# Layer 1's two h parts in one 512-column product, context's x0 by an adding DMA, and layer 1's gate sums further apart

## The chip, the cores and the metric

The kernel runs on one core of a Trainium2 chip. Its engines run side by side, each through its own list of instructions in a fixed order: TensorE (PE in the profile, with its weight loads shown apart as PEld), VectorE (DVE), ScalarE (ACT), GpSimd (POOL) and SyncE (SP), which issues nearly all DMAs. The metric is the device time of one execution in microseconds (us). Before the change it is 1170.85 us, the median of three runs (1170.73 to 1172.37).

## The reference, cut to what matters

Two layers of one block. Each layer normalises two streams of 256 tokens and 2048 features, the latents `x` and the context `ctx`, scales and shifts them, and projects both by the same `w_in` (2048 by 5120). The projection's columns feed three branches (a gated MLP, attention and a Fourier mix); their outputs, 2048 wide, go through `w_out`, are normalised, gated, and added to the stream.

```python
for l in range(DEPTH):                       # DEPTH = 2
    h   = rmsnorm(x,   g_pre[l]) * (1.0 + scale[:, None]) + shift[:, None]
    h_c = rmsnorm(ctx, g_pre[l]) * (1.0 + scale_c) + shift_c
    proj, proj_c = h @ w_in[l], h_c @ w_in[l]
    ...
    y = rmsnorm(y @ w_out[l], g_post[l])
    x_new = x + gate[:, None] * y
    if not last:
        ...                                  # the same branches on proj_c
        ctx = ctx + gate_c * y_c
    x = x_new
return x
```

In the second layer (layer 1 in the code) the context gives only keys and values to the latents' attention. So that layer needs all columns of `w_in` for 256 latent tokens, and only the columns `k` and `v` for the 256 context tokens.

## The kernel before

**Products.** Every large product is made from float32 numbers split into a high and a low part, each of a type that TensorE takes in one pass. `mm3` (L383) makes one 128-row step of a product as three matmuls into the same PSUM tile: high by high (L384), high by low (L385), low by high (L386). The low by low part is left out. In `tunit` (L473) the stationary operand is a 128 x 128 piece of the weights (`whi`, `wlo`) and the moving operand is a piece of h (`hh`, `hl`), whose columns are tokens; 16 such steps make one *unit* of 128 output features. In layer 0 a unit moves 512 columns (both streams), in layer 1 it moves the 256 latent columns, and 512 only for the two units `k`. `hh[k]` and `hl[k]` are tiles of 128 x 512: latents in the first 256 columns, context in the last 256 (`LAT`, `CTX`).

**The units of layer 1, in order.** `a_v` (h stationary, 512 columns of weights moving) together with the first two heads of `a_u` (`start_av`, `start_au`); then `au2`, `au3`; four `cx` (Fourier), four `ag` and four `cg` (gates); two `k`; `v` (h stationary, 256 columns moving); eight `q`; eight `bg`. That is 30 latent units through `tunit` and two `k` units. After that `finish` (L834) makes the output projection with tokens on the partitions and writes the result.

**Weights.** `Stream` (L331) brings 512 KB of weights at a time (half a unit) by DMA into one of three `raw` buffers; ScalarE makes the high part (`whi`, L367) and VectorE the low part (`wlo`, L368), into four buffers each, up to three halves ahead of their use.

**Order.** TensorE's instructions run in the order in which the program writes them. Work that comes back to TensorE later is a generator in `later`; each `yield d` says after how many units of a planner's clock its next piece is put between the products. `tick` advances that clock by 0.0405 per 32 moved columns of a step (0.648 per 512). The instructions of the other engines are ordered by the compiler from priorities; `low(n)` makes a block wait for the next n instructions. Delays of importance here: `YF` for the Fourier branch, `YQ, YA, YB` for attention, `YT` for `finish`.

**The context's way into layer 1.** `after_start` (L966) starts `boundary_ctx` (L980) after `au3`. It runs `boundary(1, acc)` (L908): four DMAs bring `x0` of the context into `raw` buffers; column sums of the squares of the layer's output (`col_sums`, L424) give 1/rms, spread over the partitions by `bcast` (L431); then, for each of 16 feature tiles, VectorE multiplies `yo[k]` by it (L933) and adds `x0` (L934), ScalarE squares the result (L937), and after every second tile TensorE adds the two squares into `ps_rs` (L944). Four small matmuls (L952) end the sum, and a second `bcast` gives the 1/rms of the new stream. `make_h` (L445) then writes the context halves of `hh` and `hl`. The gates `ag`, `cg` and `bg` write into the context halves of `yo`, so they follow.

**Users of a unit.** `gate` (L732), `fourier` (L615), the activation at L745 and `rope` (L644, for `q` and `k`) read the unit's PSUM tile directly. Short-lived tiles of all of them share the tag `w2k`, seven buffers (L74).

**`finish`.** `gate1` (L254) turns layer 1's gate sums, which VectorE collected in four tiles, into rows on all partitions: per 512 columns one DMA of two rows, one float32 matmul with ones (L260), an add (L261) and a product (L262) on VectorE. `turn` (L838) transposes the latents (L847) in eight pieces. Both put their products between those of `ps_y`, through the two `ms` PSUM buffers.

Of the kernel before, what the change touches and what calls it, by code (L numbers as in the profile page):

```python
# [13 lines left out]
P = 128  # L14
# [13 lines left out]
def units():  # L28
    """(name, first column, columns, first k tile, k tiles): blocks of w_in of 128 x 2048 each."""
# [37 lines left out]
def trunk_kernel(ctx: ExitStack, tc: tile.TileContext, xT, xhalf, cT, wss, wsl, wmod, win, wout0, wout1, const, vec, rows,  # L67
# [24 lines left out]
    # ---- constants  # L92
# [17 lines left out]
    class low:  # L110
        """instructions that may wait for the next `n`."""
# [22 lines left out]
    # ---- modulation: columns [128, 16, stream] of scale, shift and gate  # L134
# [5 lines left out]
    def mod_cols(l, cb, ps8):  # L140
        """ps8 [128, 4, 2]: silu(c) @ w_mod for 512 columns of column block cb."""
# [54 lines left out]
    def mod_dve(l, cb, red):  # L196
        """red [128, 2, 16]: sums over the 32 partitions of each quadrant, transposed."""
# [38 lines left out]
    def mod_gate1():  # L236
        """products of silu(c) and the gate's columns of w_mod in layer 1, still to be summed over partitions."""
# [16 lines left out]
    def gate1():  # L254
        """(sum + b_mod) * g_post of layer 1's gate, on all partitions."""
        for c in range(4):
            r = sb([P, 2, 512], F32, "mraw", 2)
            DMA.dma_start(r, rows[None, :, c * 512:(c + 1) * 512].to_broadcast([P, 2, 512]))
            ps = ms_ps("gate")
            PE.matmul(ps, ones, g1[c], start=True, stop=True)  # L260
            V.tensor_tensor(out=g1[c], in0=r[:, 0], in1=ps, op=ALU.add)  # L261
            V.tensor_tensor(out=g1[c], in0=g1[c], in1=r[:, 1], op=ALU.mult)  # L262
            yield YT

# [11 lines left out]
    YF = [5.0, 2.8], [3.8, 3.4]  # L276
# [18 lines left out]
    # ---- work of other engines that hands products back to the tensor engine later  # L295
# [32 lines left out]
    # ---- weights: raw -> exact parts hi + lo, in halves of a unit, ahead of their use  # L328
# [59 lines left out]
    def part(w, c):  # L388
        """columns c of both parts; a part is a tile or a list of tiles side by side."""
# [19 lines left out]
    # ---- per-token reciprocal rms from sums over features  # L409
# [14 lines left out]
    def col_sums(ps, q, n, start=True, stop=True):  # L424
        """columns of ps: sums over the partitions of q [128, n * 128], one accumulation group."""
# [10 lines left out]
    # ---- streams in feature-major tiles  # L436
# [7 lines left out]

    def make_h(l, k, rb, streams):  # L445
        """h = x * rstd * gs + sh, as hi + lo; rb: rstd over the tokens of `streams`."""
# [6 lines left out]
        for s in streams:  # L453
            sl = slice(s * S, (s + 1) * S)
            first = A.activation(hh[k][:, sl], t[:, sl], AF.Identity, bias=sh[l][:, k, s:s + 1])  # L455
        for s in streams:
            sl = slice(s * S, (s + 1) * S)
            last = V.scalar_tensor_tensor(out=hl[k][:, sl], in0=t[:, sl], scalar=sh[l][:, k, s:s + 1],
                                          in1=hh[k][:, sl].bitcast(F32), op0=ALU.add, op1=ALU.subtract)
# [13 lines left out]
    def tunit(n, sl=None):  # L473
        """feature-major product of one unit of 128 columns: PSUM [128, n]."""
# [8 lines left out]
        return ps  # L483

# [10 lines left out]
    # ---- one layer, up to the inputs of the output projection  # L495
    def layer(l):
# [12 lines left out]
        # a_v (token-major) and two heads of a_u, k outermost  # L509
        av = [mm_ps("av") for _ in range(nt)]  # L510
        au = [mm_ps("au") for _ in range(2)]
        def start_av(k, ts):
            c = slice((k % 2) * 512, (k % 2 + 1) * 512)
            for t in ts:
                sl = slice(t * P, (t + 1) * P)
                mm3(av[t], (hh[k][:, sl], hl[k][:, sl]), part(avw, c), k == 0, k == KT - 1)

        def start_au(k):
            for j in range(2):
                c = slice((k % 4) * 256 + j * P, (k % 4) * 256 + (j + 1) * P)  # L520
                mm3(au[j][:, 0:n], part(auw, c), (hh[k][:, 0:n], hl[k][:, 0:n]), k == 0, k == KT - 1)
# [57 lines left out]
        # branch A  # L579
        def branch_a():  # L580
            vt = [w2k([P, 512]) for _ in range(nt)]
            ss = sb([P, 4], F32, "ss")
            for j in range(2):
                A.activation(ytmp(j), au[j][:, 0:n], AF.Gelu_apprx_tanh)
# [20 lines left out]
        # branch C  # L605
# [37 lines left out]
        # branch B  # L643
        def rope(hi, lo, ps):  # L644
            """x * cos + rot(x) * sin of the latents, and x of the context, as hi + lo."""
# [10 lines left out]
            if hi.shape[-1] > S:  # L656
                split_into(hi[:, CTX], lo[:, CTX], ps[:, S:T])
# [85 lines left out]
        for h in (2, 3):  # L743
            ps = tunit(n)
# [3 lines left out]
        for g in range(4):  # L748
            ps = tunit(n)
# [3 lines left out]
        for h in range(4):  # L753
            ps = tunit(n)
            gate(h, ps)
        state["phase"] = f"cg{l}"
        for g in range(4):
            ps = tunit(n)
# [6 lines left out]
        for j in range(2):  # L765
            ps = tunit(T)
            kt.append((sb([P, T], F32R, f"kt{j}"), sb([P, T], F32R, ("ws", "bsb")[j])))
            rope(*kt[j], ps)
# [3 lines left out]
        for k in range(KT):  # L772
# [3 lines left out]
            for t in range(4):  # L776
                ts = slice(t * P, (t + 1) * P)
                mm3(vps[t][:, 0:256], (hh[k][:, ts], hl[k][:, ts]), part(w, c), k == 0, k == KT - 1)
# [3 lines left out]
        for h in range(8):  # L782
            ps = tunit(n)
# [3 lines left out]
        for h in range(8):  # L787
            ps = tunit(n)
# [11 lines left out]
    # ---- output projection  # L800
# [7 lines left out]
    def out_proj():  # L808
# [14 lines left out]
        later.add(boundary(0, acc), 1.0)  # L823
# [10 lines left out]
    def finish():  # L834
        """layer 1's output projection with tokens on partitions, and x1 + gate * y / rms(y)."""
        x1 = {}

        def turn():  # L838
            """x1 of the latents to tokens on partitions: [128, token tile, 512] per 512 columns."""
# [12 lines left out]
        later.add(turn(), 2 * YT)  # L852
# [55 lines left out]
    def boundary(s, acc):  # L908
        """x1 = x0 + gate * y / rms(y) of stream s in place, and its own 1 / rms."""
# [185 lines left out]
```

## Time and profile before

| | us |
|---|---|
| three timed runs, median (lowest to highest) | 1170.85 (1170.73 to 1172.37) |
| span of the profiled execution | 1167.9 |
| median minus that span (start and end, outside the profile) | 2.95 |
| TensorE busy in the span | 1136.0 |
| VectorE / ScalarE / GpSimd busy | 881.8 / 509.8 / 17.3 |

Layer 0 takes the span up to about 757 us, layer 1's units run from there to about 1062 us, and `finish` to the end; the context's boundary lies between 808 and 848 us, `q` between 936 and 1002 us, with attention's last pieces up to 1036 us. TensorE's granted clock is 0.996 of full speed on average. A matmul's row in the profile lasts longer than TensorE needs for it, because matmuls overlap: how long one costs is read from the distance between the starts of successive rows.

### The profile page before, as it was taken

To read this page: it belongs to the slowest core of one execution; us is meant where nothing else is said; L and a number is where in the kernel's file an instruction comes from. 1 tells how busy PE (TensorE), PEld (TensorE's weight loads), DVE (VectorE), ACT (ScalarE), POOL (GpSimd) and SP (SyncE) were. 2 spreads that over 40 slices of the span, in tenths; PEclk is the share of its full clock that TensorE was granted. 3 is DMA by queue.
4 is the path that set the end of the run, shared out by engine and by line. 5 is a ranking of instruction groups with operands and counts; after the bars stand their busy time and mean duration, and the time that the engine had idled before them with its cause. 6 is when DMAs were issued, how large, how long until landed. Compare 5 with 4: busy or idle time off the path is not lost.

```text
span 1167.9 us, 17483 instructions
## 1 busy us (share of the span) xinstructions
PE 1136.0 (97%) x6656; PEld 953.7 (82%) x6656; DVE 881.8 (76%) x1469; ACT 509.8 (44%) x914; POOL 17.3 (1%) x23
## 2 busy tenths in 40 slices
PE   3999999999999999999999999999999999999996
PEld 1466688888898888888888888889899999997885
DVE  5454498888988878798989886495896678888554
ACT  4222513322224667632533233365563278745442
POOL 0000000000000000000000000200000000000001
PEclk9999999999999999999999999999999999999998
DMA  9999765466665334455466665365656665688563
GB/s 339 378 387 357 254 196 166 145 202 193 200 200 178 105 114 136 134 175 173 158 199 209 205 216 162 109 207 173 205 158 205 203 200 178 195 269 244 190 187 120
DMA packets 73892, 234.32 MB, mean 201 GB/s; under 512 B 8528, under 2 KB 9680, under 8 KB 73808
## 3 DMA queue, kind: packets, MB, share of 16 engines
q1 hardware_dynamic: 73808, 233.21, 61.6%
q8 instruction: 52, 0.85, 0.3%
q14 instruction: 32, 0.26, 0.1%
HBM read 231.08 MB, written 2.10 MB: 200 GB/s over the span
## 4 chain that ended last, share of the span: by engine, by line
PE 92%; DVE 3%; DMA 2%; ACT 2%; issue 1%; POOL 0%; SPq 0%; DVEq 0%; ACTq 0%; POOLq 0%
PE ps_t L384 20%; PE ps_t L385 20%; PE ps_t L386 20%; PE ps_mod L172 3%; PE ps_av L384 2%; PE ps_y L386 2%; PE ps_y L384 2%; PE ps_y L385 2%; PE ps_av L385 2%; PE ps_av L386 2%; PE ps_v L386 1%; PE ps_v L384 1%; PE ps_v L385 1%; PE ps_tp L722 1%; PE ps_au L384 1%
## 5 line engine op out<-in xcount | busy, mean ns | idle before, releaser
L384 PE MATMUL ps_t<-hh,whi 128*128 128x512 f32 (+1 forms) x1296 | 452.1, 349 | 0.0
L386 PE MATMUL ps_t<-hh,wlo 128*128 128x512 f32 (+1 forms) x1296 | 447.4, 345 | 0.0
L385 PE MATMUL ps_t<-hl,whi 128*128 128x512 f32 (+1 forms) x1296 | 447.0, 345 | 0.0
L367 ACT CAST whi<-raw 128x1024 fp32r<-128x1024 f32 x218 | 228.2, 1050 | 397.3 <-PE ps_t L385 274.4
L368 DVE TENSOR_TENSOR wlo<-raw,whi 128x1024 fp32r<-128x1024 f32 x218 | 265.3, 1220 | 99.1 <-ACT whi L367 98.8
L384 PEld LDWEIGHTS ps_t<-hh,whi 128*128 128x128 f32 x1296 | 244.9, 189 | 34.3 <-issue 4.6
L386 PEld LDWEIGHTS ps_t<-hh,wlo 128*128 128x128 f32 x1296 | 244.7, 189 | 30.6
L385 PEld LDWEIGHTS ps_t<-hl,whi 128*128 128x128 f32 x1296 | 244.9, 189 | 28.9 <-issue 0.5
L209 DVE SCALAR_TENSOR_TENSOR macc<-mraw,cs,macc 128x512 f32<-128x512 f32 x360 | 249.9, 745 | 17.6 <-DMA mraw<-in_wmod_dram 17.5
L455 ACT ACTIVATE hh<-w2k,sh 128x256 fp32r<-128x256 f32 x64 | 29.0, 502 | 61.4 <-DVE w2k L451 61.4
L384 PE MATMUL ps_y<-whi,hh 128*128 128x512 f32 x112 | 45.0, 401 | 0.0
L386 PE MATMUL ps_y<-whi,hl 128*128 128x512 f32 x112 | 43.8, 392 | 0.0
L385 PE MATMUL ps_y<-wlo,hh 128*128 128x512 f32 x112 | 43.7, 390 | 0.0
L384 PE MATMUL ps_av<-whi,hh 128*128 128x512 f32 x96 | 40.0, 416 | 0.0
L385 PE MATMUL ps_av<-wlo,hh 128*128 128x512 f32 x96 | 37.9, 395 | 0.4 <-DVE wlo L368 0.4
L172 PE MATMUL ps_mod<-hh,kt 128*32 128x512 f32 x64 | 21.5, 649 | 17.0 <-DMA hh<-in_wss_dram 17.0
L386 PE MATMUL ps_av<-whi,hl 128*128 128x512 f32 x96 | 37.6, 392 | 0.0
L386 PE MATMUL ps_v<-whi,hl 128*128 128x256 f32 x128 | 36.2, 283 | 0.0
L384 PE MATMUL ps_v<-whi,hh 128*128 128x256 f32 x128 | 36.2, 283 | 0.0
L385 PE MATMUL ps_v<-wlo,hh 128*128 128x256 f32 x128 | 36.2, 283 | 0.0
L468 DVE TENSOR_TENSOR acc<-acc,w2k 128x512 f32<-128x512 f32 (+1 forms) x33 | 21.2, 641 | 18.7 <-ACT w2k L467 17.2
L401 ACT CAST w2k<-ps_tp 128x512 fp32r<-128x512 f32 x40 | 23.5, 587 | 22.8 <-PE ps_scc L385 12.0
(292 smaller groups left out, 1491.8 us busy)
## 6 DMA issues: line engine op xcount, KB each, us to landing
raw<-in_win_dram SPq DMA_DIRECT2D x160, 512.0 KB, 4.1
mraw<-in_wmod_dram SPq DMA_DIRECT2D x128, 512.0 KB, 4.3
raw<-in_wout_dram SPq DMA_DIRECT2D x64, 512.0 KB, 4.2
hh<-in_wss_dram SPq DMA_DIRECT2D x32, 256.0 KB, 5.6
hl<-in_wss_dram SPq DMA_DIRECT2D x32, 256.0 KB, 5.4
yo<-in_xT_dram SPq DMA_DIRECT2D x16, 256.0 KB, 5.4
mraw<-in_wsl_dram SPq DMA_DIRECT2D x8, 512.0 KB, 6.9
yo<-in_wsl_dram SPq DMA_DIRECT2D x16, 256.0 KB, 7.2
```

Source lines behind the costliest of these rows:

```text
L172: PE.matmul(ps[32 * kk:32 * kk + 32, 0:n], cpad[:, kg * 4 + kk], ws[kk], start=kg == 0, stop=kg == 3, tile_position=(0, 32 * kk))
L209: V.scalar_tensor_tensor(out=acc[:, s], in0=w[:, kk % 2], scalar=c, in1=acc[:, s], op0=ALU.mult, op1=ALU.add)
L367: A.copy(ph, r[:, c])
L368: self.last = V.tensor_tensor(out=pl, in0=r[:, c], in1=ph.bitcast(F32), op=ALU.subtract)
L384: PE.matmul(ps, st[0], mv[0], start=start, stop=False)
L385: PE.matmul(ps, st[0], mv[1], start=False, stop=False)
L386: PE.matmul(ps, st[1], mv[0], start=False, stop=stop)
L401: A.copy(hi, src)
L455: first = A.activation(hh[k][:, sl], t[:, sl], AF.Identity, bias=sh[l][:, k, s:s + 1])
L468: V.tensor_tensor(out=acc[:, sl], in0=acc[:, sl], in1=q[:, sl], op=ALU.add)
L722: PE.transpose(tp[:, (2 * j + b) * P:(2 * j + b + 1) * P], src, ident)
```

## The change

1. In layer 1, `hh[k]` holds the latents' high part and low part side by side (256 + 256 columns), and `hl[k]` the same for the context (`h_of`). A latent step is then two matmuls (`mm2`): `whi` by all 512 columns, and `wlo` by the high part, added to the first 256 columns. Afterwards `joined` copies the second half of the PSUM tile to a `w2k` tile on ScalarE and adds the first half on VectorE. All 30 latent units, the two heads in `start_au`, and the two `k` units (as two PSUM tiles, one per stream) go this way; `a_v` and `v` keep `mm3`.
2. The context's boundary has its own `boundary_ctx`: `x0` is no longer loaded into `raw` and added by VectorE, but added in place by 16 DMAs of 128 KB that GpSimd issues; the squares are summed by VectorE in a tile `acc1`, four tiles behind (`LATE`), and `col_sums` of that tile replaces the matmuls L944 and L952.
3. `gate1` takes a step every 6.0 of the planner's clock in place of 2.0, `turn` every 3.0 in place of 2.0; layer 1's Fourier delays grow by 0.8 each.

Comments and docstrings also go. The diff, cut to its core:

```diff
-    YF = [5.0, 2.8], [3.8, 3.4]
+    YF = [5.0, 2.8], [4.6, 4.2]
-    YT = 2.0
+    YT, YG = 3.0, 6.0
     YH = 2.0
-    NX = [4, 2]
-    YX, YR = [1.0, 2.0], 0.8
+    NX, LATE = 4, 4
+    YX, YR, YC, YE = 1.0, 0.8, 1.6, 2.0
...
+    def h_of(l, k, sl):
+        if l == 0:
+            return hh[k][:, sl], hl[k][:, sl]
+        s, a = sl.start // S, sl.start % S
+        t, b = (hh, hl)[s][k], a + sl.stop - sl.start
+        return t[:, a:b], t[:, S + a:S + b]
...
+    def mm2(ps, w, h, k):
+        PE.matmul(ps, w[0], h, start=k == 0, stop=False)
+        PE.matmul(ps[:, 0:S], w[1], h[:, 0:S], start=False, stop=k == KT - 1)
+
+    def joined(ps):
+        t = w2k([P, S])
+        A.copy(t, ps[:, S:T])
+        V.tensor_tensor(out=t, in0=t, in1=ps[:, 0:S], op=ALU.add)
+        return t
+
+    def tunit1(streams):
+        pss = [mm_ps("t") for _ in streams]
+        for k in range(KT):
+            if k % 8 == 0:
+                w = W.next()
+            for s, ps in zip(streams, pss):
+                mm2(ps, part(w, slice((k % 8) * P, (k % 8 + 1) * P)), (hh, hl)[s][k], k)
+                later.tick(PASS * S)
+        return [joined(ps) for ps in pss]
...
         for h in range(8):
-            ps = tunit(n)
+            ps = tunit1([0])[0] if last else tunit(n)
             later.add(attention(h, ps))
...
-            yield YT
+            yield YG
...
-        later.add(turn(), 2 * YT)
+        later.add(turn(), 1.5 * YT)
...
+    def boundary_ctx(acc):
+        r = sb([P, S], F32, "rbs", 2)
+        r0 = yield from rms_of(1, acc[:, CTX], 2.2)
+        A.copy(r, r0)
+        acc1 = sb([P, S], F32, "acc1")
+        for k in range(KT + LATE):
+            if k < KT:
+                V.tensor_tensor(out=yo[k][:, CTX], in0=yo[k][:, CTX], in1=r, op=ALU.mult)
+                G.dma_start(yo[k][:, CTX], xhalf[1, k // 4][:, k % 4], accum_op=ALU.add)
+            i = k - LATE
+            if i >= 0:
+                q = w2k([P, S]) if i else acc1
+                A.activation(q, yo[i][:, CTX], AF.Square)
+                if i:
+                    V.tensor_tensor(out=acc1, in0=acc1, in1=q, op=ALU.add)
+            if k % 2:
+                yield YC
+        yield YE
+        r0 = yield from rms_of(1, acc1, 2.6)
+        r = sb([P, S], F32, "rbs", 2)
+        V.tensor_copy(r, r0)
+        for i, k in enumerate(ORDER):
+            make_h(1, k, r, [1])
+            state["ctx"].append(k)
+            if i % 2:
+                yield YH
...
-        yield from lowered(boundary(1, state["acc"]))
...
+            later.add(lowered(boundary_ctx(state["acc"])))
```

`rms_of(s, acc, wait)` is the first half of the old `boundary`: column sums of `acc`, 1/rms, and after `wait` the `bcast`.

More of the change, by code (lines that the diff above doesn't have):

```diff
@@ L583, in branch_a @@
             for j in range(2):
-                A.activation(ytmp(j), au[j][:, 0:n], AF.Gelu_apprx_tanh)
+                A.activation(ytmp(j), joined(au[j]) if last else au[j], AF.Gelu_apprx_tanh)
             for t in range(nt):
@@ L748, in layer @@
         for g in range(4):
-            ps = tunit(n)
+            ps = tunit1([0])[0] if last else tunit(n)
             later.add(fourier(g, ps))
@@ L753, in layer @@
         for h in range(4):
-            ps = tunit(n)
+            ps = tunit1([0])[0] if last else tunit(n)
             gate(h, ps)
@@ L757, in layer @@
         for g in range(4):
-            ps = tunit(n)
+            ps = tunit1([0])[0] if last else tunit(n)
             gate(12 + g, ps)
@@ L782, in layer @@
         for h in range(8):
-            ps = tunit(n)
+            ps = tunit1([0])[0] if last else tunit(n)
             later.add(attention(h, ps))
@@ L787, in layer @@
         for h in range(8):
-            ps = tunit(n)
+            ps = tunit1([0])[0] if last else tunit(n)
             if h == 7:
@@ L822, in out_proj @@
             o_evac(j, ps, yo[j], acc, [0], False)
-        later.add(boundary(0, acc), 1.0)
+        later.add(boundary(acc), 1.0)
         for j in range(KT - HELD, KT):
@@ L906, in trunk_kernel, with rms_of, boundary @@
     rbs = {}
-    def boundary(s, acc):
-        sl = slice(s * S, (s + 1) * S)
+    def rms_of(s, acc, wait):
+        ps = ms_ps("rs")
+        col_sums(ps, acc, 2)
+        dg = rstd_diag(ps[:, 0:2], 2, D)
+        yield wait
+        return bcast(dg, 2)[:, 0:S]
+    def boundary(acc):
         x0s = []
```

74 lines of the change are left out of this document (32 added, 42 removed).

## The prediction

> **What bounds the kernel now.** I read the page first, then the windows of layer 1, then TensorE's timeline for the distance between starts, and last the waits.
>
> ```profile
> span 1167.9 us, 17483 instructions
> PE 1136.0 (97%) x6656; PEld 953.7 (82%) x6656; DVE 881.8 (76%) x1469; ACT 509.8 (44%) x914; POOL 17.3 (1%) x23
> ...
> PE 92%; DVE 3%; DMA 2%; ACT 2%; issue 1%; POOL 0%; SPq 0%; DVEq 0%; ACTq 0%; POOLq 0%
> ```
>
> TensorE carries 92% of the chain that ends last, so a matmul taken away counts in full unless another engine is close behind. One place is like that (windows; columns: us, then busy us of each engine):
>
> ```profile
> 995.00:1005.00 10.00, 9.91 (x78) 9.44 (x77) 8.94 (x17) 8.56 (x18) 0.00 (x0) 1.00 0.48 151
> ...
> 1015.00:1025.00 10.00, 9.54 (x79) 9.28 (x78) 9.66 (x18) 6.99 (x14) 0.00 (x0) 1.00 0.69 234
> ```
>
> Here, beside layer 1's attention, VectorE is busy for 8.9 to 9.7 of 10 us and ScalarE for 7.0 to 8.6. The chain in order of time leaves TensorE from 968.8 to 1017.1 us, which spans the five units q5, q6, q7, bg0, bg1. The waits there:
>
> ```profile
> PEld ps_o L385 <- DVE w2k L402: 2.9, 5, 1.2
> ...
> PE ps_o L385 <- DVE w2k L402: 1.7, 3, 1.0
> ```
>
> What a product costs, by its start (first column), in a stage of 512 columns and in one of 256:
>
> ```profile
> 270.12 0.40 PE L385 MATMUL ps_t<-hl,whi 128*128 128x512 f32 x1
> ...
> 275.81 0.39 PE L386 MATMUL ps_t<-hh,wlo 128*128 128x512 f32 x1
> ...
> 861.74 0.28 PE L384 MATMUL ps_t<-hh,whi 128*128 128x256 f32 x1
> ...
> 868.20 0.28 PE L384 MATMUL ps_t<-hh,whi 128*128 128x256 f32 x1
> ```
>
> 25 steps take 5.69 us, 0.2276 each; 54 steps take 6.46 us, 0.1196 each. Twice 0.1196 is 0.2392: a product has a fixed part of about 0.0116 us beside its columns. The granted clock is 1.00 in both stages.
>
> **1. The joined product.** A latent step goes from 3 x 0.1196 = 0.3588 to 0.2276 + 0.1196 = 0.3472 us, 0.0116 less: the columns stay 768, one fixed part goes. 30 units x 16 plus 2 x 16 steps of `a_u` are 512 steps: 5.9 us. The two `k` units go the other way: 3 x 0.2276 becomes 2 x 0.3472, 0.0116 more, times 32 steps: 0.4 us. Net gain 5.5 us. Smaller end: in the stage of `a_v` 512-column products follow each other by 0.2325 (762.16 to 762.63 us); with that a step gains 0.0067, net 3.2 us. Larger end: 0.116 is seen for a 256 that is followed by a 512, net 7. I take 5.5, from the stages that are made of units alone.
>
> [...]
>
> Weight loads fall from three to two per step. A load lasts 190 ns in the trace but overlaps, and 128-column transposes, each with its own load, start 0.11 us apart; so loads did not set the 0.1196, and nothing more is gained from them.
>
> **2. `joined`, per unit.** One ScalarE copy out of PSUM (0.373 us, as L730) and one VectorE add (0.418, as L654): 36 of each (30 units, two heads of `a_u`, two streams of two `k` units): 13.4 us on ScalarE, 15.0 on VectorE.
>  - `au`, `cx`, `ag`, `cg`, `k`: hidden. From 808 to 900 us VectorE is busy for about 78%, and TensorE waits for neither engine. The Fourier's first product came 2.0 us after its input (819.24, 821.28); `joined` takes 0.8 and the delay grows by 0.8 of the planner. Without that cover it is 0.8 us per `cx`, 3.2 in all.
>  - `q`: the scores' product starts 2.1 and 1.9 us after the low part of q is ready (991.54 to 993.64; 1001.72 to 1003.62), so 0.8 fits. But VectorE's list gets longer. In the five units where the chain already runs through it I put the add on the path: 5 x 0.418 = 2.1 us lost, and TensorE's gain there, 5 x 16 x 0.0116 = 0.9, is not cashed. Ends: 0, if the idle 10% takes it and the order of the lists improves (then even the 2.9 us of waits could go); and all 16 units of `q` and `bg` at 0.79 each, 12.7 us, if copy and add both lie on the chain, where `w2k`, seven tiles, gets one more user per unit.
>  - `bg`: VectorE is at 8.3 to 9.1 of 10 us, with TensorE waiting for nothing; `out0` in layer 0 ran at 38.16 of 40 (560 to 600 us) without TensorE waiting, so 95% is bearable. Nothing charged.
>
> **3. The context's sums.** Eight groups like this leave TensorE:
>
> ```profile
> 814.13 0.28 PE L386 MATMUL ps_t<-hh,wlo 128*128 128x256 f32 x1
> 814.34 0.63 PE L944 MATMUL ps_rs<-w2k,ones 128*32 128x256 f32 x4
> 814.90 0.38 PE L384 MATMUL ps_t<-hh,whi 128*128 128x256 f32 x1
> 815.12 0.28 PE L385 MATMUL ps_t<-hl,whi 128*128 128x256 f32 x1
> ```
>
> From 814.13 to 815.12 it is 0.99 us, without the group two steps of 0.12: 0.75 us, times 8: 6.0. The four L952 cost 0.69 - 0.24 = 0.45 (843.19 to 843.88), and the `col_sums` in their place 0.91 - 0.24 = 0.67 like the first ones (808.00 to 808.91): 0.2 back. Net gain 5.8 us. VectorE trades 16 adds of `x0` for 15 adds of squares: equal. SP loses four 512 KB loads, which held `raw` buffers; no wait of TensorE came from these, so 0.
>
> New is the path of the sum: product on VectorE, DMA issued by GpSimd, square, add. TensorE needs it at the second `col_sums`, 18.0 planner units after the first `bcast`. L952 stood 16.8 after it, 32.0 us later (811.3 to 843.3), so 18.0 are 34.3 us, less 6.0 and 1.0 of gains: it is due at 838.6. The first product is done at 812.8. Less 4.5 for a landing (the 128 KB loads of `w2k` from `const`) and 0.95 for square, add and hand-over, 20.4 us are left for 16 issues: 1.27 us each. What GpSimd takes for an issue no row shows. Nearest rows: 0.70 us (L414, its smallest instruction) and 0.85 (L934, 128x256); upper end 5.4, if each waited for the landing of the one before (256 KB loads). GpSimd's list holds nothing else there but the power (L414) of the second sum, last behind the 16. On VectorE only the product waits, for the `bcast`, as before. ScalarE's list now holds squares that wait for a landing, with weight casts (`whi`) and Fourier copies behind them; the casts run up to three halves ahead, some 8 us of TensorE's work, and cover a late square. I take 0.85 to 1.0, hidden, price 0.
>
> **4. `finish`.** Transposes wait for a PSUM buffer that holds a gate sum, whose add waits for VectorE or for the rows' DMA (6.3 us):
>
> ```profile
> 1068.59 1.02 PE L260 MATMUL ps_gate<-ctrl,ones 128*128 128x512 f32 x2
> 1070.33 0.66 PE L847 MATMUL ps_x<-identr,yo 128*128 128x128 f32 x4 [0.72 <-DVE ctrh L261]
> ```
>
> 1.74 us against 0.86 for two products of 0.43: 0.9 lost here, 0.5 more at 1077.64. Gate sums 6 planner units apart leave room for a DMA and an add: gain 1.4 us. Ends 0 and 1.4.
>
> **Sum.** 5.5 + 5.8 + 1.4 - 2.1 - 0.9 = 9.7 us off the profiled span of 1167.9; the 2.95 us by which the runs' median exceeds it stay. 1170.85 - 9.7 = 1161.
>
> **Rivals.**
>  - *VectorE takes over from `q` to the end.* For it: its 9.66 of 10 us. Against it: TensorE ran unhindered beside 95% in layer 0. With the add alone on the path in all 16 units: 6.7 us lost instead of 2.1, 3.0 us of TensorE's gain instead of 0.9: 1168. With the copy too (12.7): 1174.
>  - *The adding DMAs come late: slower.* One mechanism: GpSimd spends p per issue, the 16 go one after another, and TensorE stands before the second `col_sums`. Above p = 1.27 it costs 16 (p - 1.27); 9.7 us, the whole gain, are gone at p = 1.88, and at 2.5 it ends at 1181. For it: nothing in the trace excludes it. Against it: the rows of 0.70 and 0.85. [...]
>  - *In alternation the fixed part does not go away*: the weights for a 512-column product must now load behind one of 256 alone, so each pair loses what it saved. For it: 0.2325 between 512-column products in the stage that mixes both sizes. Against it: in that stage the start after the last 512 comes 0.23 later and that after the last 256 0.12 (761.22, 761.45; 762.04, 762.16). With a tenth of a microsecond per unit less than forecast (net 2.2 of the 5.5) it is 1164.4, with nothing of the joining 1166.
>  - *Nothing is gained*, because TensorE is made to wait elsewhere for each removed piece: 1168.5 to 1173. Against it: from 808 to 960 us its waits are only 0.1 to 0.2 us at a switch of kind.
>
> **Chances.** The forecast (1157 to 1164): 0.58. VectorE with the add: 0.12, with the copy too: 0.03. Alternation: 0.09. Nothing gained: 0.04. DMAs late: 0.07 with part of the gain left (1161 to 1168.5), 0.07 beyond. A change within 0.2%, 2.3 us, is about what runs of this kernel can't tell from none. Faster: 0.58 + 0.12 + 0.09 + 0.04 (the earlier half of the late DMAs with part of the gain) = 0.83; the same: 0.04 + 0.03 = 0.07; slower: 0.07 + 0.03 = 0.10. The range: the low end from the larger joining gain (7.0), sums 6.0, gates 1.4 and 2.0 of the 2.9 us of waits, with nothing charged, 16.4: 1154.5; the high end takes in VectorE with the add and the alternation: 1168.5.
>
> **What the changed profile would show.** Right: layer 1's `ps_t` rows alternate 128x512 and 128x256, a pair every 0.347 us; a `cg` unit lasts 5.55 us, not 5.73; no L944 group between 812 and 842 us of layer 1; no wait of L847 on a gate's add; waits of `ps_o` on L402 of about 5 us. Wrong: a pair at 0.355 or more, a gap before the second `ps_rs`, GpSimd busy above 20 us there, `whi` waiting behind a square, or waits of `ps_sc` on q's parts.

## The result: slower by 0.33%, and the profile after

The changed kernel takes 1175.52 us (median of 20 runs, 1171.54 to 1180.06) against 1171.56 us of the kernel before (20 runs, 1170.09 to 1173.68). The ratio is 1.0033, with a 95% interval of 1.0021 to 1.0044. The forecast was 1161.0 us, with a range to 1168.5. It was wrong in sign.

The profiled execution after took 1172.25 us; its span is 2.6 us longer than that of before. In every run of the experiments and of the kernel after the time lies 1.7 to 1.9 us above the span, so both profiled executions were among the fastest of their kernel (that of before took some 1169.7 us), and the 2.95 us of the table ahead of the prediction are not start and end alone. From the page of after:

```profile
span 1170.5 us, 16589 instructions
PE 1129.3 (96%) x6146; PEld 928.2 (79%) x6146; DVE 893.6 (76%) x1503; ACT 519.6 (44%) x950; POOL 32.9 (3%) x39
...
PE 87%; DMA 3%; DVE 3%; ACT 3%; issue 2%; POOL 1%; SPq 0%; DVEq 0%; ACTq 0%; POOLq 0%
```

TensorE is busy for 6.7 us less. But its share of the chain that ends last falls from 92% to 87%, and DMA, ScalarE and GpSimd take over: TensorE has less to do and waits more.

In what follows, `ps_rs` are column sums and `ps_rb` the broadcast of a 1/rms; `ps_mix` is the gated MLP's mixing product, `ps_f` and `ps_z` are the first and the second product of a Fourier unit, `ps_sc` and `ps_o` attention's scores and output, `ps_x` the transposes and `ps_y` the output projection. Line numbers are those of each run's own kernel. A wait outside a fence is counted by starts: how much later a product starts than the one ahead of it would have let it (0.12 us after 256 columns, 0.23 after 512).

I set the starts of layer 1's units of both traces side by side (the time from the first product of each stage on TensorE to that of the next, us):

| stage | before | after | difference |
|---|---|---|---|
| `av`, `au2` | 41.80 | 41.46 | -0.34 |
| `au3` | 6.61 | 7.35 | +0.74 |
| `cx0` to `cx2` | 25.08 | 24.49 | -0.59 |
| `cx3`, `ag0` | 17.43 | 22.74 | +5.31 |
| `ag1` to `cg3` (7 units) | 40.86 | 40.21 | -0.65 |
| `k0`, `k1` | 21.88 | 22.58 | +0.70 |
| `v`, `q0` to `q4` | 58.51 | 58.14 | -0.37 |
| `q5` | 11.39 | 9.51 | -1.88 |
| `q6` to `bg7` | 79.30 | 78.67 | -0.63 |
| first `ps_y` to the end | 105.64 | 106.01 | +0.37 |

So the loss sits in `cx3` and `ag0`, beside the context's second statistic, and everything else together gains 2.6 us. Three readings follow.

*The joined product.* TensorE's timeline in the `ag` and `cg` units of after (first column: start, us):

```profile
867.72 0.40 PE L496 MATMUL ps_t<-hh,whi 128*128 128x512 f32 x1
867.95 0.28 PE L497 MATMUL ps_t<-hh,wlo 128*128 128x256 f32 x1
...
882.87 0.40 PE L496 MATMUL ps_t<-hh,whi 128*128 128x512 f32 x1
```

43 pairs lie between the two 512-column starts: 15.15 us, 0.352 us each, where I had forecast 0.347 and three products took 0.359. A unit of 16 steps goes from 5.73 to 5.64 us: 0.09 us, half of the 0.186 forecast.

*The second broadcast.* The last product ahead of the second `ps_rb` (L433) starts at 847.62; the broadcast starts at 851.33, 3.58 us late. The chain in order of time (start, length, what):

```profile
847.13 1.06 ACT whi L367
...
848.21 0.03 DVE wlo L368
848.24 1.11 issue
849.35 0.50 DVE w2k L659 x2
...
849.92 0.41 ACT w2k L401
...
850.36 0.42 DVE w2k L402
850.78 0.41 DVE w2k L421 x2
851.19 0.14 issue
851.33 0.67 PE ps_rb L433 x2
```

The power on GpSimd (L414) was done at 846.56 us, so the diagonal (L421) could have been made then. But in VectorE's list it stands behind a `wlo` (L368) and a Fourier unit's subtraction and low part (L659, L402). (One more `wlo`, an L402 and a join's add stand there too, but were done by 846.5.) This `wlo` needs a `whi` that ScalarE could only begin at 847.13, when a product of TensorE had given its buffer free. TensorE's next products stand behind the broadcast. So the wait is nearly a ring: from the freed buffer through ScalarE, VectorE, ScalarE and VectorE back to TensorE, 4.2 us. In the trace of before only one L402 stands between the statistic (L412) and L421, and the broadcast waits for nothing. VectorE's rows of before, and the L412 of after:

```profile
844.39 0.14 DVE L412 TENSOR_SCALAR rs_a<-ps_rs 128x2 f32<-128x2 f32 x1
845.01 0.43 DVE L402 TENSOR_TENSOR w2k<-w2k,w2k 128x256 fp32r<-128x256 f32 x1 [0.48 <-ACT w2k L401]
845.40 0.49 DVE L421 TENSOR_SCALAR w2k<-identr,rs_b 128x128 f32<-128x128 f32 x2
...
844.67 0.16 DVE L412 TENSOR_SCALAR rs_a<-ps_rs 128x2 f32<-128x2 f32 x1 [0.43 <-PE ps_rs L429]
```

*The Fourier branch.* The chain from an adding DMA to a late product of the second Fourier unit (`cx1`):

```profile
830.07 0.87 POOL yo L1005
830.94 1.66 issue
...
832.61 4.37 DMA yo<-in_xhalf_dram
...
837.06 0.04 ACT w2k L1009
...
837.38 1.04 ACT whi L367
...
838.44 1.23 DVE wlo L368
839.67 0.20 DVE w2k L402
...
839.91 0.40 PE ps_z L386
```

The DMA's landing holds a square (L1009) at the head of ScalarE's list; a weight cast, its low part and Fourier's L402 stand behind it, and TensorE waits for these. Between 800 and 850 us ScalarE waited 7.3 us for adding DMAs, and TensorE was busy for 41.86 of 50 us (50.00 of 50 in the same stretch of before).

### The profile page after: what moved, and what is told of

The parts are those of the page before. It is cut to its first block, busy times and chain, and to the rows that moved or that the text cites. A ratio compares the mean times of both kernels' runs of the same rounds, so it can differ in the third digit from the quotient of the medians.

```text
span 1170.5 us, 16589 instructions
## 1 busy us (share of the span) xinstructions
PE 1129.3 (96%) x6146; PEld 928.2 (79%) x6146; DVE 893.6 (76%) x1503; ACT 519.6 (44%) x950; POOL 32.9 (3%) x39
## 4 chain that ended last, share of the span: by engine, by line
PE 87%; DMA 3%; DVE 3%; ACT 3%; issue 2%; POOL 1%; SPq 0%; DVEq 0%; ACTq 0%; POOLq 0%
PE ps_t L384 15%; PE ps_t L385 15%; PE ps_t L386 15%; PE ps_t L496 7%; PE ps_t L497 3%; PE ps_mod L172 3%; PE ps_y L386 2%; PE ps_y L384 2%; PE ps_y L385 2%; PE ps_av L384 2%; DMA mraw<-in_wmod_dram 2%; PE ps_av L385 2%; PE ps_av L386 2%; PE ps_v L386 1%; PE ps_v L384 1%
## 5 line engine op out<-in xcount | busy, mean ns | idle before, releaser
L368 DVE TENSOR_TENSOR wlo<-raw,whi 128x1024 fp32r<-128x1024 f32 x218 | 265.3, 1220 | 90.2 <-ACT whi L367 89.1
L384 PE MATMUL ps_t<-hh,whi 128*128 128x512 f32 (+1 forms) x784 | 301.0, 384 | 0.0
L386 PE MATMUL ps_t<-hh,wlo 128*128 128x512 f32 (+1 forms) x784 | 299.4, 382 | 0.0
L385 PE MATMUL ps_t<-hl,whi 128*128 128x512 f32 (+1 forms) x784 | 299.1, 382 | 0.0
L496 PE MATMUL ps_t<-hh,whi 128*128 128x512 f32 x512 | 185.8, 401 | 0.0
L385 PEld LDWEIGHTS ps_t<-hl,whi 128*128 128x128 f32 x784 | 147.4, 188 | 27.3 <-issue 0.2
L497 PE MATMUL ps_t<-hh,wlo 128*128 128x256 f32 x512 | 143.5, 280 | 0.0
L463 ACT ACTIVATE hh<-w2k,sh 128x256 fp32r<-128x256 f32 x48 | 21.7, 501 | 56.9 <-DVE w2k L459 56.9
```

The costliest lines, as they stand in the source:

```text
L368: self.last = V.tensor_tensor(out=pl, in0=r[:, c], in1=ph.bitcast(F32), op=ALU.subtract)
L384: PE.matmul(ps, st[0], mv[0], start=start, stop=False)
L385: PE.matmul(ps, st[0], mv[1], start=False, stop=False)
L386: PE.matmul(ps, st[1], mv[0], start=False, stop=stop)
L463: first = A.activation(h_of(l, k, sl)[0], t[:, sl], AF.Identity, bias=sh[l][:, k, s:s + 1])
L496: PE.matmul(ps, w[0], h, start=k == 0, stop=False)
```

## The experiments

Each time is compared with runs of the kernel before on the same chip, in between. "Span" is of the profiled execution (before: 1167.9 us).

| run | what it is | median us | span | ratio to before (95%) |
|---|---|---|---|---|
| e3 | before + new gate delays | 1167.78 | 1166.0 | 0.9975 (0.9965 to 0.9986) |
| e2 | before + new context boundary | 1171.74 | 1167.2 | 1.0009 (0.9998 to 1.0020) |
| e13 | before + new `YF` | 1175.51 | 1173.1 | 1.0035 (1.0024 to 1.0046) |
| e14 | before + join, old `YF` | 1174.68 | 1172.9 | 1.0026 (1.0017 to 1.0035) |
| e1 | before + join + new `YF` | 1183.32 | 1182.1 | 1.0102 (1.0084 to 1.0119) |
| e6 | before + context + gates | 1168.43 | 1166.7 | 0.9978 (0.9969 to 0.9987) |
| e10 | before + context + gates + new `YF` | 1175.29 | 1171.8 | 1.0042 (1.0026 to 1.0059) |
| e9 | after, old `YF` | 1173.29 | 1172.2 | 1.0019 (1.0008 to 1.0030) |
| e4 | after, diagonal on GpSimd, broadcast later | 1170.40 | 1171.5 | 0.9997 (0.9983 to 1.0010) |
| e5 | after, `x0` added on VectorE | 1177.60 | 1171.6 | 1.0042 (1.0026 to 1.0057) |
| e8 | after, squares 8 tiles behind | 1170.63 | 1167.7 | 1.0001 (0.9991 to 1.0010) |
| e15 | after, profiled again | 1174.97 (one run) | 1173.2 | |
| e7 | after, join only in `cg`, `k`, `q`, `bg0` to `bg6` | 1174.96 | 1172.8 | 1.0035 (1.0022 to 1.0048) |
| e11 | e6, squares 8 tiles behind | 1169.11 | 1166.0 | 0.9986 (0.9977 to 0.9995) |
| e12 | e11 + join as in e7 | 1167.50 | 1165.2 | 0.9975 (0.9964 to 0.9986) |
| e16 | e3 + join in `cg`, `k`, `q`, `bg0` to `bg5` | 1167.48 | 1165.0 | 0.9963 (0.9951 to 0.9975) |
| e17 | e3 + join in `cg`, `k`, `q` | 1166.08 | 1164.4 | 0.9948 (0.9934 to 0.9962) |

### One part alone: gates, context, join with its delays (e3, e2, e1)

e3 has the lines with `YT, YG` and `1.5 * YT` of the change, e2 its `rms_of`, `boundary`, `boundary_ctx` and their constants, and e1 the rest, the join with the new `YF`, beside the old `boundary`, `boundary_ctx` and gate delays:

```diff
 # e1, against the kernel after
-    YT, YG = 3.0, 6.0
+    YT = 2.0
-        later.add(turn(), 1.5 * YT)
+        later.add(turn(), 2 * YT)
-            later.add(lowered(boundary_ctx(state["acc"])))
+            later.add(boundary_ctx())
```

> The kernel after with the context's boundary and layer 1's gate sums put back as they were: the joined products alone (with h_of and the new YF). Theory A (the loss is made at the context's boundary): the join alone gains what the units showed, about 0.09 us for each of some 30 units less 0.35 us for each k unit, so 2 us: ratio to before 0.997 to 0.999, TensorE's stalls between 800 and 850 us as small as before (about 5 us), no 3-us wait ahead of the second ps_rb. Rival B (the join's extra copies on ScalarE and adds on VectorE make the lists late, and the context's work only shows it): same or slower than before, 1.000 to 1.003, with the stall ahead of the second ps_rb there without any adding DMA.

> The kernel before with the new context boundary alone (x0 by adding DMAs, squares summed on VectorE), products by three and gates as before. Theory A: it carries the loss: 6.0 us of L944 products go, some 8 us of new stalls of TensorE come between 800 and 850 us (3 to 4 us of them ahead of the second ps_rb), so the profiled span is 1.5 to 3 us longer than before and the ratio 1.002 to 1.006. Rival B: without the join's work on ScalarE and VectorE the lists are on time: faster by 3 to 6 us, 0.995 to 0.997.

> The kernel before with the new delays of layer 1's gate sums and of the transposes of x alone. Theory A: the 1.4 us of waits on the gates' adds go, and nothing else moves, since the wait of the first ps_y product on the low part of y came with the shorter q and bg units: 0.998 to 0.9995. Rival C (the spread gates put that wait there): no gain, a wait of L386 on the subtraction of L835 as in the kernel after, 0.9995 to 1.001.

The gates gain 1.9 us of span, 1.7 of them behind the first `ps_y` (105.64 to 103.92 us), a little more than A allowed; C falls. The context alone changes nothing that can be measured, where A had a loss and B a gain. The join with its delays loses 12.7 us, far more than the whole change; so A falls, and B holds in its direction at over three times its price. The waits of e1 between 800 and 860 us:

```profile
PE ps_rs L981 <- ACT w2k L974: 4.7, 2, 4.4
...
PE ps_rb L433 <- DVE w2k L421: 3.7, 2, 3.1
```

No adding DMA is in this kernel. The old sums on TensorE wait for squares, and the second broadcast for its diagonal.

### Join or delays? (e6, e10, e13, e14, e9)

My next theory was that the join's copy and add, two more changes of engine per unit, make the lists late. e6 takes the join out of the kernel after, with its delays; e10 then puts the delays back, e13 is one line, e14 the join without that line, e9 the kernel after without it:

```diff
 # e13, against the kernel before (e10: the same line, on e6; e9: the reverse, on the kernel after)
-    YF = [5.0, 2.8], [3.8, 3.4]
+    YF = [5.0, 2.8], [4.6, 4.2]
```

> The kernel before with the new context boundary and the new gate delays: the kernel after without its join. Theory F (the join's copy and add put two more engine changes between a unit's products and its user, and ScalarE's and VectorE's lists, which run in order, pass the delay on): the waits of 0.8 us at ps_mix and at the first ps_rb and of 3.6 us at the second ps_rb go, the wait of the first ps_y on the low part of y goes, and the span is 5 us below the profiled run of the kernel after: ratio to before 0.997 to 0.999. Rival A (the context boundary itself makes the loss): the 3.6-us wait stays, ratio 0.9995 to 1.002.

> The kernel before with the new context boundary, the new gate delays and the new YF, no join. Theory Y: a wait of 2 to 4 us ahead of the second ps_rb comes back without any join, and in part of the runs a lowered clock behind it: 2 to 5 us above the kernel with the old YF, ratio to before 0.9995 to 1.002. Rival F: no such wait, ratio 0.997 to 0.9985.

> The kernel before with one line changed: layer 1's Fourier delays 4.6, 4.2 instead of 3.8, 3.4. Theory Y (the delays alone do it): Fourier's pieces move past the context's second statistic, a wlo stands ahead of the diagonal L421 in VectorE's list, and the second ps_rb waits 1.5 us or more: ratio to before 1.001 to 1.004. Rival J (only with the join's work are the lists late): no such wait, 0.999 to 1.0005.

> The kernel before with the join alone, all else as before, YF too. Rival J (two more steps on ScalarE and VectorE for each Fourier unit): the waits of Fourier's products and of the context's sums on ScalarE and VectorE between 800 and 860 us come to 6 us or more, ratio 1.002 to 1.008. Theory Y (the delays do it): under 3 us of such waits, the units' 0.09 us show, 0.998 to 1.000.

> The kernel after with the old delays of layer 1's Fourier pieces (YF 3.8, 3.4 instead of 4.6, 4.2). Theory Y (the longer delays alone put a second wlo into VectorE's list ahead of the diagonal L421, and that wlo needs a whi whose buffer TensorE frees only just before the broadcast): the 3.6-us wait ahead of the second ps_rb goes although every unit is still joined; the Fourier waits grow by up to 2 us, since the joined unit's two extra steps now stand in a shorter delay; span 1.5 to 3.5 us below the profiled run of the kernel after, ratio to before 0.998 to 1.0005. Rival F (the join's copy and add make it late): the wait of 2.5 us or more stays, ratio 1.002 or more.

Without join and delays the kernel is 0.22% faster than before; with the delays alone on top it is 0.42% slower; and the delays alone, on the kernel before, cost 4.0 us. Nothing on any engine has become more in e13: the same instructions stand in another order. The chain of e13 ahead of its second broadcast is that of after in small:

```profile
845.97 1.06 ACT whi L367
...
847.05 1.23 DVE wlo L368
848.27 0.34 DVE w2k L402
848.61 0.41 DVE w2k L421 x2
849.01 0.14 issue
849.15 0.67 PE ps_rb L433 x2
```

A `wlo` has got in between L412 and L421 there; in e10, as in after, two have. The stall is 2.2 us in e13, 2.5 in e10, and in e10 Fourier's `ps_f` waits 4.9 us before it. So Y holds, and in e10 the price is over twice what it allowed (1.0042 against 1.002 at most): 0.8 of the planner's clock more between Fourier's pieces puts them, and with them the weights' parts, beside the second statistic.

The delays are not all of it. The join alone, with the old delays (e14), loses 3.1 us by the medians (5.0 by the spans), and rival J holds too by its ratio, although its 6 us of waits between 800 and 860 us are not reached. They are 4.7 us, in no single stall: 0.8 us each at `ps_mix` and at the first `ps_rb`, 2.5 us at the sums L981, 0.6 at the second `ps_rb`. Another 4.0 us are lost from the first `ps_y` to the end. There the gates' old delays stand, and the waits from 1058 to 1090 us are:

```profile
PE ps_x L884 <- DVE ctrh L261: 2.2, 1, 2.2
...
PE ps_y L386 <- DVE hl L835: 1.9, 1, 1.9
```

And e9 fails the expectation of Y: with join and old delays the second broadcast waits 0.9 us only, but Fourier's `ps_f` waits 2.3 and 3.4 us, since the joined unit now comes late for them. So the longer delays and the join each cost, each in its own way, and the prices don't add up: together they take 12.7 us on the old boundary and 6.4 on the new one (1.0033 against e6's 0.9978).

### What in the kernel after? (e4, e5, e8, e11, e15)

```diff
 # e4: L421 of the second context statistic on GpSimd, behind the pow
-            V.tensor_scalar(out=dg[:, j], in0=ident, scalar1=r[:, j:j + 1], scalar2=None, op0=ALU.mult)
+            eng.tensor_scalar(out=dg[:, j], in0=ident, scalar1=r[:, j:j + 1], scalar2=None, op0=ALU.mult)
-        r0 = yield from rms_of(1, acc1, 2.6)
+        r0 = yield from rms_of(1, acc1, 4.5, G)
 # e5: x0 loaded into raw as before
-                G.dma_start(yo[k][:, CTX], xhalf[1, k // 4][:, k % 4], accum_op=ALU.add)
+                V.tensor_tensor(out=yo[k][:, CTX], in0=yo[k][:, CTX], in1=x0s[k // 4][:, k % 4], op=ALU.add)
 # e8 on the kernel after, e11 on e6
-    NX, LATE = 4, 4
-    YX, YR, YC, YE = 1.0, 0.8, 1.6, 2.0
+    NX, LATE = 4, 8
+    YX, YR, YC, YE = 1.0, 0.8, 1.25, 2.0
```

> The kernel after, where the diagonal of the context's second 1/rms is made on GpSimd, right behind the pow, instead of in VectorE's list, and the broadcast comes 1.9 us of the planner's clock later. Theory A with a clock effect (the 3.6-us stall of TensorE also lowers the granted clock in most executions): the stall goes (3 us or more), the granted clock is above 0.995 in nearly all runs, and the time falls by 5 to 7 us below the kernel after, to a ratio to before of 0.997 to 0.999. Theory A without it: the stall goes, the spread of the times and of the clocks stays, 2.5 to 3.6 us below the kernel after, 0.9995 to 1.001. Rival D (TensorE then waits for the next late thing): under 1.5 us gained.

> The kernel after with x0 brought by SP into the raw buffers and added on VectorE as in the kernel before; the squares are still summed on VectorE. Theory F: the adding DMAs cost only what ScalarE's squares wait for them, some 9 us of ScalarE's waits; with VectorE's 16 adds of 0.34 us (5.4 us) more in its list, the Fourier waits of 0.5 to 1.4 us between 820 and 842 us get no smaller, and the wait ahead of the second ps_rb stays over 2 us: within 2 us of the kernel after, ratio to it 0.999 to 1.002. Rival H (the adding DMAs are what makes the lists late): those waits fall below 1 us in sum, the 3.6-us wait goes, 4 us or more below the kernel after.

> The kernel after with each square taken eight tiles behind its adding DMA instead of four, the steps 1.25 instead of 1.6 us of the planner's clock apart, so that the second statistic comes at nearly the same place. Rival H: ScalarE's waits of 9 us for the adding DMAs go to under 2 us and with them the Fourier waits and the late second broadcast: 4 us or more below the kernel after. Theory F: ScalarE's waits for the DMAs go, but the 3.6-us wait and the ps_mix and first ps_rb waits stay; 0 to 2 us below the kernel after.

> The kernel before with the new context boundary and the new gate delays, each square eight tiles instead of four behind its adding DMA (steps of 1.25 instead of 1.6 us of the planner's clock). If the 4.5 us of Fourier waits that the context boundary brings without any join come from ScalarE's squares that wait for the adding DMAs at the head of its list, they go to under 2 us: span 1163 to 1164.5, ratio to before 0.994 to 0.996. If they come from the mass of the squares and adds on ScalarE and VectorE, they stay above 3 us: 0.997 to 0.9985.

> The kernel after, unchanged, profiled once more. If the spread of its runs comes from the granted clock, a run of over 1174 us shows a stretch of 5 us or more at about half clock behind the stalls at 835 to 851 us, and its length accounts for what it is above 1172 us; its stalls are those of the first profile. If the time differs without such a stretch, the spread has another cause.

e4: the stall goes (3.58 to 0.50 us) and its lowest time (1168.14) lies 3.4 us below the lowest of after; the ratio falls by 0.0036, to 0.9997. That is A without the clock effect. The spread stays, and the profiled execution shows where: it lost elsewhere what it had gained (windows; the third number from the end is the granted clock):

```profile
835.00:840.00 5.00, 3.55 (x21) 2.82 (x19) 3.47 (x7) 2.08 (x6) 1.83 (x3) 1.00 0.90 187
840.00:845.00 5.00, 4.38 (x17) 3.60 (x18) 3.61 (x11) 2.63 (x8) 0.00 (x0) 0.60 0.55 157
845.00:850.00 5.00, 5.00 (x19) 4.46 (x18) 1.82 (x4) 0.99 (x3) 1.57 (x1) 0.50 0.23 46
850.00:855.00 5.00, 4.66 (x25) 3.89 (x24) 2.17 (x4) 2.11 (x5) 1.29 (x2) 0.87 0.30 88
```

Behind a stretch with 71% of TensorE busy the clock falls to 0.60 and 0.50; 5.2 us of full clock are missing (1 minus the clock, times 5 us, summed), which would be half clock for some 10 us. e15, the kernel after once more, has the same stalls (3.58 us at the broadcast), and behind them 0.76 and 0.90 in the windows from 850 and 855: 1.7 us missing. It took 2.7 us longer than the first profile, which has none; Fourier's waits, 0.7 us longer in sum, are most of the rest.

e5: F holds. Without adding DMAs the kernel is no faster, Fourier waits 4.4 us in one piece and the broadcast 2.6. Adding on VectorE or by DMA is not the point. e8: ScalarE's waits for the DMAs stay (6.9 us against 7.3), which both theories had wrong; the new distances put the second statistic ahead of Fourier's piece, the 3.6-us wait goes, and one of 2.8 us at the `col_sums` themselves comes; the ratio falls by 0.0032 all the same. On e6 (e11) the same edit brings nothing. Why squares eight tiles behind still wait for their DMAs, the traces tell in part: the edit hardly moved the first of them. In after as in e8 ScalarE starts the first square at 819.2 us, at the landing of its own DMA, when VectorE has done eight products; the next three start within 0.4 us of those in after, and 5.3 of the 6.9 us of waits are at these four. So the order that the compiler made shows little of the longer distance, and e8 and e11 hardly test it.

### The join where its user can wait (e7, e12, e16, e17)

`tunit3` is a unit by three products, read from PSUM directly; the new layout of h stays.

```diff
+    def tunit3():
+        ps = mm_ps("t")
+        for k in range(KT):
+            if k % 8 == 0:
+                w = W.next()
+            mm3(ps[:, 0:S], part(w, slice((k % 8) * P, (k % 8 + 1) * P)), h_of(1, k, LAT), k == 0, k == KT - 1)
+            later.tick(PASS * S)
+        return ps
 # cx, as in au2, au3, ag; start_au likewise; bg7 in e7 and e12, bg6 and bg7 in e16, all bg in e17
-            ps = tunit1([0])[0] if last else tunit(n)
+            ps = tunit3() if last else tunit(n)
```

> The kernel after with products by three, read from PSUM directly as before, in the first two heads of a_u, au2, au3, cx0 to cx3, ag0 to ag3 and the last bg unit; the join stays in cg, k, q and bg0 to bg6. Theory F: none of the join's waits is left (ps_mix, both ps_rb, the first ps_y), each of the 19 single units still gains 0.09 us and each k unit still loses 0.35 us, so it is 1 us below the kernel without the join: ratio to before 0.996 to 0.998. Rival G (what costs is the new layout of the high and low parts or the load of the engines as a whole, not where the join sits): a stall of over 1.5 us in ag0 or at the first ps_y stays, 0.999 or more.

> The same as the kernel without the join and with squares eight tiles behind, but with the join in cg, k, q and bg0 to bg6 (not in a_u, cx, ag and the last bg). Theory: where a unit's user is not urgent the join is worth its 0.09 us a unit (19 of them, 1.7 us) less 0.35 us for each k unit: 1.0 us below that kernel, and no new wait. Rival (the joined bg units make h_lo of the out-projection late): the first ps_y waits 0.5 us or more on the subtraction of L835 and nothing is gained.

> The kernel before with the new gate delays, and the join in cg, k, q and bg0 to bg5 alone (Fourier delays and context boundary as before). If the join is worth its 0.09 us a unit where the user isn't urgent: 18 units gain 1.6 us, two k units lose 0.7 us, the gates gain 1.9 us: span 1164.5 to 1165.5, ratio to before 0.996 to 0.9975, no wait of the first ps_y over 0.5 us. If joined units cost elsewhere, no better than the gate delays alone: 0.9975 or more.

> The kernel before with the new gate delays and the join in cg, k and q alone, so with no joined bg unit. If joined bg units are what makes the last h_lo late (a wait of 1.55 us of the first ps_y on L844 with the join in bg0 to bg5), that wait goes and the six bg units lose 0.09 us each: 1.0 us below the kernel with them, span 1164, ratio to before 0.9945 to 0.9965. If the wait stays, its cause is elsewhere in VectorE's list, and the time is 0.5 us above that kernel.

e7 kept the new delays, and keeps the stalls (4.6 us at `ps_f`, 2.0 at the second broadcast, then a granted clock of 0.51 and 0.50 from 840 to 850 us) without a joined product near: what first spoke for G was, by e10 and e13, the delays. With the old ones e12 is 0.8 us of span below e11 (1.0 forecast), e16 is 1.0 us below e3 (0.9 forecast). But in e16 the first `ps_y` waited 1.55 us for the low part of y, and 0.9 in e12. e17 has no joined `bg` unit; the wait is gone, first `ps_y` to the end takes 103.9 us as in e3, and its median is the lowest of all, 0.52% below the kernel before. That it is the joined `bg` units which make y's low part late is thereby shown.

That e12 and e16 came out near their forecasts is luck, and the 1.6 us of span by which e17 lies below e3 are not the price of a product. Unit by unit, the two `k` units lose 0.7 us, `cx3`, which is not joined, loses 0.5, and eleven of the twelve joined single units gain 0.8 together. What carries the gain is the twelfth, `q5`, with 1.88 us: in e3 two of its `ps_o` products are 1.1 and 0.5 us late for VectorE's L402, and these waits are gone. `q5` gains the same 1.9 us in after, e1, e7, e12, e14 and e16. So here too it is a wait for VectorE that decides, this time the right way; why the join takes it away is open. No run left the join out of the `k` units alone, where it loses.

## Why the prediction was wrong, step by step

Forecast were 9.7 us less, measured 3.9 us more. By the ratios, the context's boundary and the gates together gave 2.6 us (e6) where 7.2 were forecast, and the join with its delays took 6.4 on top of that where 2.5 of gain were forecast (5.5 less the 2.1 and 0.9 of `q` and `bg`). So 8.9 of the 13.6 us lie in the second part.

- **The cover of `joined` in `au`, `cx`, `ag`** failed, and it carries most of the error. I wrote "hidden", because "TensorE waits for neither engine" and because the delay grows by 0.8 of the planner's clock where `joined` takes 0.8 us. I priced the longer delay at nothing, as a cushion. It is a move: it shifts Fourier's pieces against the second statistic in VectorE's ordered list, and alone it costs 4.0 us (e13). The join alone costs 3.1 (e14). VectorE's 78% was the wrong row to read; the right one was what stands between L412 and L421 in its list.
- **The context's sums, 5.8 us**, were not cashed. The L944 groups are gone, but e2 ran from `cx0` to the end of `ag0` only 0.3 us faster. TensorE gave the rest back in Fourier's products: 1.1 us at a `ps_f`, 2.1 in three at a `ps_z`, 1.2 at a later `ps_f`, and 1.0 in waits of 0.3 us or less beside them. "Hidden, price 0" looked at the second `col_sums`, which indeed waited for nothing; but the Fourier copies behind a late square were not covered, and the chain of after shows the sign that I had named as wrong, a `whi` behind a square. The landing took 6.6 us at the median, where I put 4.5, up to 9.2 for the ten that GpSimd issued in a row, and 4.4 and 8.2 us on the chains of after and e2.
- **The rival of late adding DMAs** had the place wrong (Fourier through ScalarE's list, not the second `col_sums`). GpSimd was busy for 16.75 of 50 us, under the bound of 20 named as wrong; 14.5 of these are the 16 issues, 0.9 us each, as I had taken. The adding DMAs are not alone the cause (e5).
- **The join's 5.5 us**: a size. 0.09 us a unit and 0.35 us lost per `k` unit make about 2.0. That is the alternation rival, half way: the mean distance is 0.234 us after a 512-column product and 0.118 after one of 256, and the pair takes 0.352. Whether the weight loads set these distances was not shown.
- **The `q` and `bg` stages**: the 3.0 us charged there were not paid. VectorE did not take over:

```profile
995.00:1005.00 10.00, 9.99 (x63) 8.79 (x62) 7.92 (x16) 8.39 (x18) 0.00 (x0) 1.00 0.45 124
...
1015.00:1025.00 10.00, 9.25 (x58) 7.95 (x57) 9.20 (x19) 8.39 (x20) 0.00 (x0) 1.00 0.71 233
```

  The waits of `ps_o` for L402 fell from 1.7 us to 0.3 instead of rising to 5, and `q5` gained 1.88 us: the end named as possible ("then even the 2.9 us of waits could go"). That it would come was not forecast, and its cause stays open.
- **The gates' 1.4 us** were right, 1.7 alone (e3). In the kernel after they are paid for by a wait that I did not name, of the first `ps_y` on the low part of y (1.6 us), which the joined `bg` units bring (e17).
- **The median against the profile**: I left the distance between span and median at 2.95 us. After has 5.0; the forecast has no term for the clock. In e15, 2.7 us above the first profile, a lowered clock behind the stalls makes 1.7 of these. The granted clock on record for each run says more: 1 minus the clock, times the span, is 8.1 us in the mean of after's 20 runs, against 4.1 in e6 and 4.0 in the runs of before that the experiments list. So up to 4.0 of the 6.4 us above e6 go with a lowered clock, though a single run need not follow it (one of 1176.98 us had 0.996). Where in those runs the clock fell was not profiled.

## What to carry to other kernels

Where engines work through ordered lists, a longer delay for one task is not a cushion but a new order (one line of delays cost 4.0 us in e13): before you price it at nothing, write down what then stands ahead of the next instruction that TensorE waits for, and whether something in that row itself waits for TensorE. A cheaper product that adds a copy and an add was worth its gain here only where the unit's user was not urgent: in 12 single units, and not near a statistic, a transform or the last unit of a phase. Even there its 0.09 us a unit were less than one wait that came or went with the order. And stalls cost twice where the clock fell behind them (5.2 us of full clock in e4's profile, 1.7 in e15's), so compare medians of many runs and not one profile.

## What the runs showed of the hardware

- **A lowered granted clock behind stalls, in nine of eleven profiles.** In before, e2, e3, e6, e11, e12, e16 and e17 the granted clock is 1.00 from 835 to 860 us; in e11 it is 0.82 and 0.84 in the two windows from 825 us, with waits of 0.8 and 1.0 us there. Of the eleven profiles with a wait of over 1.5 us or several near 1 us there, nine show a granted clock between 0.50 and 0.90 in one to four windows of 5 us; the first profile of after and e14 show none. In e7, behind 4.6 us of waiting, it is 0.51 from 840 to 845 us and 0.50 from 845 to 850. In e4, where no single wait was longer than 1.6 us, it is 0.60 and 0.50 in the same two windows. With the same 3.58 us of waiting at the broadcast, e15 has 0.76 and 0.90 in the two windows from 850 us and the first profile of after 1.00: what decides between them was not shown. The missing clock (1 minus the clock, times 5 us, summed) is 1.7 us each in e11 and e15, and 5.2 in e4.
- **A 256-column product between two of 512 columns** starts 0.234 us after the one ahead, and the next one 0.118 us after it (means of 43 pairs in the `ag` and `cg` units of after), so the pair takes 0.352 us where 0.2276 + 0.1196 are 0.347.
- **An adding DMA of 128 KB** issued by GpSimd landed after 6.6 us (median of 16) in after and 7.0 in e2, counted from the start of its issue; ten in a row started 0.55 us apart in six of nine gaps and 0.75 to 1.44 in the others, and the late ones of these took up to 9.2; one of 512 KB from SP, for the latents' `x0`, took 4.6 in after.
